# The value projections of a hybrid attention encoder in two groups of 512 columns instead of three of 384, 384 and 256

## The chip, the core and the metric

The kernel runs on one core of a Trainium2 chip. The metric is device time in microseconds of one execution, here the median of three runs. The engines are named as the profile names them: PE (TensorE, matrix products; PEld is its loading of weights), DVE (VectorE), ACT (ScalarE), POOL (GpSimd) and SP (SyncE, which issues the loads).

## The reference

Two layers over 256 tokens of width 1024, in float32. Each layer is a feed-forward block at half weight, a token-mixing block and a second feed-forward block, each with an RMS norm ahead of it and one behind it. The mixing block has one input projection that is split into three groups of heads: A (6 heads, banded attention with a bias), B (4 heads, differential attention) and C (6 heads, stick-breaking attention).

```python
proj = h @ w_in
sizes = [WIDTH_A, WIDTH_A, WIDTH_A, B_QK_WIDTH, B_QK_WIDTH, WIDTH_B, WIDTH_C, WIDTH_C, WIDTH_C]
qa, ka, va, qb, kb, vb, qc, kc, vc = jnp.split(proj, [int(c) for c in np.cumsum(sizes)[:-1]], axis=-1)
o_a = chunk_band_attention(qa.reshape(hd_a), ka.reshape(hd_a), va.reshape(hd_a), rel_bias)
...
o_b = diff_attention(qb.reshape(hd_bqk), kb.reshape(hd_bqk), vb.reshape(b, s, N_HEADS_B, DIFF_V_DIM),
                     lam, subln_g, lambda_init)
...
o_c = stick_breaking_attention(qc.reshape(hd_c), kc.reshape(hd_c), vc.reshape(hd_c))
y = jnp.concatenate([o_a.reshape(b, s, WIDTH_A), o_b.reshape(b, s, WIDTH_B),
                     o_c.reshape(b, s, WIDTH_C)], axis=-1)
return y @ w_out
```

The values va (384 columns), vb (256) and vc (384) are 1024 columns together.

## The kernel before

**Split products.** Each float32 product is made of three passes of rounded operands: a weight is cut into a rounded part (`whi`, by ACT, line 136) and the rest (`wlo`, the difference, by DVE, line 137), the activations likewise, and `mm3` (lines 366 to 368) multiplies high by high, high by low and low by high. Activations stand transposed in `xT`, K-tile by K-tile (8 of them), for two token tiles of 128 tokens.

**The stream of weights.** `Stream` holds all weights of the kernel as a list of chunks of up to 1152 columns, in the order of their use. `load` fetches a chunk into one of four raw buffers from SP's queue. `ahead(n)` issues the cutting of the next n half chunks, each one cast on ACT and one subtraction on DVE; when a chunk's second half has been cut, the chunk four places behind it is loaded. It stops where nine chunks are cut and not yet used (up to three more, "spare", lie in tiles that the feed-forward block has left free, in the trace under the names hh and hl). `done` gives a chunk back. All this is issued in program order: each engine takes its instructions in the order in which the code issued them, so where `ahead` stands in the code decides what a cast stands behind on ACT and a subtraction on DVE.

**The values.** In a mixing block of the first layer the values take chunks 66 to 73: chunks of 3, 3 and 2 K-tiles for C, the same for A, and two of 4 K-tiles for B. `values(g, t)` multiplies one group for one token tile into a PSUM tile (`pv`, named in the order of instructions by layer, group and token tile, so pv0_1_0 is layer 0, group 1, tile 0) and copies it to `v`, on ACT, for group 1 on DVE. The order is group 0 tile 0, group 1 tile 0, group 0 tile 1, group 1 tile 1, group 2 for both. In group 1 tile 0, ahead of its last chunk, `turn1` is called: it transposes the second token tile's normed activations (`pt`, line 361) and splits them into `xT` (lines 304 and 305).

**The projections and the attention.** Sixteen tiles of queries and keys follow (`pp`, chunks 74 to 89 in the first layer, one chunk of 128 columns each), and the heads' attention is dealt out among them by a table, `PLAN`: each tile has four slots, numbered through from 0 to 63, and an event at 15.4 is issued behind the matmuls of slot 15. Names used below: the first two B heads' scores `s_b` and softmaxes `p_b` (lines 854, 855, 830, 832) stand in slot 15 and those of the other two in slot 24; `wT_b` is the copy on ACT of a head's transposed weights (line 844) and `o_b` the product with the values that reads it (line 884); `z_c` and `yb` are a pair of C heads (lines 778 to 786). `PLAN["pieces"]` has the argument of `ahead` for each slot:

```python
"pieces": [
    1, 0, 0, 1, 2, 0, 3, 0, 0, 2, 1, 0, 2, 0, 0, 4, 0, 0, 0, 4, 0, 0, 2, 2, 2, 1, 0, 2, 4, 3, 1, 1, 1,
```

Of the kernel before, what the change touches and what calls it, by code (L numbers as in the profile page):

```python
# [9 lines left out]
F32 = mybir.dt.float32  # L10
# [6 lines left out]
P = 128  # L17
# [8 lines left out]
QA, KA, VA = 0, 384, 768  # L26
QB, KB, VB = 1152, 1408, 1664
QC, KC, VC = 1920, 2304, 2688
YA, YB, YC = 0, 384, 640
EPS = 1e-6  # L30
NEG = -1e30
FAR = 1e30
# [128 lines left out]
def trunk_kernel(  # L161
    ctx: ExitStack,
    tc: tile.TileContext,
    x, x_cols, f1_pre, f1_gate, f1_up, f1_down, f1_post,
    m_pre, w_in, rel_map, lq1, lk1, lq2, lk2, sub_g, w_out, m_post,
    f2_pre, f2_gate, f2_up, f2_down, f2_post,
    out,
):
    nc = tc.nc
# [8 lines left out]
    psum = ctx.enter_context(tc.tile_pool(name="psum", bufs=4, space=bass.MemoryType.PSUM))  # L178
# [40 lines left out]
    stream = Stream(nc, raw_pool, split_pool)  # L219

    def rows(ap, l, k0, k1, c0, c1):
        return ap[l, k0 * P : k1 * P, c0:c1].rearrange("(k p) n -> p k n", p=P)
# [13 lines left out]
        for k in range(KF):  # L236
            stream.add(rows(down, l, k, k + 1, 0, D), 1, D)

    V_CUTS = ((0, 3), (3, 6), (6, 8))
    QK_TILES = (  # L240
        [c for j in range(2) for c in (QB + j * P, KB + j * P)]
        + [c for j in range(3) for c in (QC + j * P, KC + j * P)]
# [2 lines left out]
    OUT_ORDER = [5, 6, 7, 3, 4, 0, 1, 2]  # L245

    def plan_mix(l):
        for c in (VC, VA):
            for k0, k1 in V_CUTS:
                stream.add(rows(w_in, l, k0, k1, c, c + 384), k1 - k0, 384)  # L250
        for h in range(2):
            stream.add(rows(w_in, l, 4 * h, 4 * h + 4, VB, VB + 256), 4, 256)
        for c in QK_TILES:
            stream.add(rows(w_in, l, 0, KT, c, c + P), KT, P)
        for k in OUT_ORDER:
            stream.add(rows(w_out, l, k, k + 1, 0, D), 1, D)
# [110 lines left out]
        nc.tensor.matmul(ps, lhsT=ah, rhs=bl, start=False, stop=False)  # L367
        nc.tensor.matmul(ps, lhsT=al, rhs=bh, start=False, stop=last)  # L368

    def tokens_out(ps, chunks, t, between=None):  # L370

        k, total = 0, sum(stream.src[c][1] for c in chunks)
        for c in chunks:
            if between and c == chunks[-1]:
                between()
            wh, wl = stream.get(c)
            for j in range(stream.src[c][1]):
                mm3(ps, xT[:, k, 0, t, :], xT[:, k, 1, t, :], wh[:, j, :], wl[:, j, :], k == 0, k == total - 1)
                k += 1

    def cols_out(ps, c, quarter=lambda q: None):

        wh, wl = stream.get(c)
        for k in range(KT):
            mm3(ps, wh[:, k, :], wl[:, k, :], xT[:, k, 0], xT[:, k, 1], k == 0, k == KT - 1)
            if k % 2:
                quarter(k // 2)
# [298 lines left out]
    def mix(i, l, turn1):  # L686
        lam_init = 0.8 - 0.6 * math.exp(-0.3 * l)
        v = act.tile([P, 2, D], F32, tag="bigl2", name=f"v{l}")
        big2 = act.tile([P, 6, SEQ], F32, tag="bigh2", name=f"big2_{l}")
        alibi, dist, dneg = big2[:, :NH_B, :], big2[:, 4, :], big2[:, 5, :]  # L690
# [10 lines left out]
        def make_lambda():  # L701
            for m in range(2):
# [9 lines left out]


        c = stream.used
        vgroups = [(YC, [c, c + 1, c + 2], 384, "acc"), (YA, [c + 3, c + 4, c + 5], 384, "acc"),
                   (YB, [c + 6, c + 7], 256, "rot")]

        def values(g, t, between=None):
            y0, chunks, n, tag = vgroups[g]
            pv = psum.tile([P, 512], F32, tag=tag, name=f"pv{l}_{g}_{t}")  # L720
            tokens_out(pv[:, :n], chunks, t, between)
            (nc.scalar.copy if g != 1 else nc.vector.tensor_copy)(v[:, t, y0 : y0 + n], pv[:, :n])

        values(0, 0)
        stream.ahead(2)
        values(1, 0, turn1)
        stream.ahead(2)
        nc.scalar.preload_act_table_set("natural_log_exp_and_others")
        values(0, 1)
        stream.done(3)  # L730
        stream.ahead(6)
        values(1, 1)
        stream.done(3)
        stream.ahead(6)
        values(2, 0)
        values(2, 1)
        stream.done(2)
        stream.ahead(6)
        qkT = act.tile([P, 16, SEQ], F32, tag="bigh1", name=f"qkT{l}")
        yb = act.tile([P, 2816], F32, tag="bigl1", name=f"yb{l}")  # L740
        yB = yb[:, :512].rearrange("p (t d) -> p t d", t=2)
# [11 lines left out]
        def pair_c(j):  # L753


            nm = f"c{l}_{j}"
            fq, fk = 4 + 2 * j, 5 + 2 * j
            zt = work.tile([P, D], F32, tag=("xg", "gpre")[j % 2], bufs=1, name=f"z_{nm}")
            z = zt[:, :768]
            if j % 2:  # L760
                e = work.tile([P, D], F32, tag="fg", bufs=1, name=f"e_{nm}")[:, :768]
            else:
                e = yb[:, 2048:2816]


            def cuts(x):
                return x[:, :512].rearrange("p (h t) -> p h t", h=2), x[:, 512:768].rearrange("p (h t) -> p h t", h=2)

            z0, z1 = cuts(z)
            for h in range(2):  # L770
                b = 64 * h
                q, k = qkT[b : b + 64, fq, :], qkT[b : b + 64, fk, :]
                s = psum.tile([P, 384], F32, tag="acc", name=f"s_{nm}_{h}")
                nc.tensor.matmul(s[:, 0:256], lhsT=k[:, 0:P], rhs=q, start=True, stop=True)
                nc.tensor.matmul(s[:, 256:384], lhsT=k[:, P:SEQ], rhs=q[:, P:SEQ], start=True, stop=True)

                diag = zt[:, 256 * h :][:, : 2 * (512 - 128 * h)].rearrange("p (b t) -> p b t", b=2)[:, :, :P]
                nc.vector.tensor_add(diag, s.rearrange("p (b t) -> p b t", t=P)[:, 0:3:2, :],
                                     negmask.unsqueeze(1).broadcast_to([P, 2, P]))
                nc.vector.tensor_copy(z0[:, h, P:], s[:, P:256])  # L780
                yield
            nc.scalar.activation(e, z, AF.Abs)
            nc.scalar.activation(e, e, AF.Exp, scale=-1.0)
            nc.scalar.activation(e, e, AF.Ln, bias=1.0)
            yield
            nc.vector.scalar_tensor_tensor(e, z, 0.0, e, ALU.max, ALU.add)
            yield
            h0 = work.tile([P, 512], F32R, tag="ta", bufs=TA, name=f"h0_{nm}")
            l0 = work.tile([P, 512], F32R, tag="tc", bufs=3, name=f"l0_{nm}")
            hl1 = work.tile([P, 512], F32R, tag="tb", bufs=3, name=f"hl1_{nm}")  # L790
            h1, l1 = hl1[:, :256], hl1[:, 256:]
            nc.scalar.copy(h1, e[:, 512:])
            nc.scalar.copy(h0, e[:, :512])
            nc.vector.tensor_sub(l1, e[:, 512:], h1.bitcast(F32))
            nc.vector.tensor_sub(l0, e[:, :512], h0.bitcast(F32))
            yield
            u1 = psum.tile([P, 256], F32, tag="acc", name=f"u1_{nm}")
            nc.tensor.matmul(u1, lhsT=tri, rhs=h1, start=True, stop=False)
            nc.tensor.matmul(u1, lhsT=tri, rhs=l1, start=False, stop=True)
            u0 = psum.tile([P, 512], F32, tag="acc", name=f"u0_{nm}")  # L800
            nc.tensor.matmul(u0, lhsT=tri, rhs=h0, start=True, stop=False)
            nc.tensor.matmul(u0, lhsT=tri, rhs=l0, start=False, stop=False)
            late = u0.rearrange("p (h t) -> p h t", h=2)[:, :, P:]
            for x, stop in ((h1, False), (l1, True)):
                nc.tensor.matmul(late, lhsT=ones_r, rhs=x.rearrange("p (h t) -> p h t", h=2), start=False, stop=stop)
            yield
            nc.vector.tensor_sub(z[:, 512:], z[:, 512:], u1)
            nc.vector.tensor_sub(z[:, :512], z[:, :512], u0)
            yield
            nc.scalar.activation(e, z, AF.Exp)  # L810
            yield
            o = psum.tile([P, SEQ], F32, tag=where("oC"), name=f"o_{nm}")
            e0, e1 = cuts(e)
            for h in range(2):
                vs = slice(YC + 64 * (2 * j + h), YC + 64 * (2 * j + h) + 64)
                columns_out(o, h, v[:, :, vs], e0[:, h, :], e1[:, h, :])
            yield
            if not yC:

                yC.append(act.tile([P, 6, SEQ], F32R, tag="bigh2", name=f"yC{l}"))  # L820
            split_copy(yC[0][:, j, :], yC[0][:, 3 + j, :], o)
            yield
# [35 lines left out]
        def head_b(h):  # L858
            fq, fk = 2 * (h // 2), 2 * (h // 2) + 1
            ps = []  # L860
# [14 lines left out]
                nc.vector.scalar_tensor_tensor(p0[:, a:b], p1[:, a:b], fac[:, t : t + 1], p0[:, a:b],  # L875
                                               ALU.mult, ALU.add)
            yield
            vs = slice(YB + 64 * h, YB + 64 * h + 64)
            pT = turned(f"b{l}_{h}", p0)
            yield  # L880
            w = turned_copy(f"b{l}_{h}", pT)
# [26 lines left out]
        def pair_a(j):  # L908
# [9 lines left out]
            ps = [soft(nms[m], ss[m], biasA[:, 2 * j + m, :], "ta") for m in range(2)]  # L918
# [10 lines left out]
            yield  # L929
            o = psum.tile([P, SEQ], F32, tag="rot", name=f"o_{nms[0]}")  # L930
            for m in range(2):
                vs = slice(YA + 64 * (2 * j + m), YA + 64 * (2 * j + m) + 64)
                columns_out(o, m, v[:, :, vs], ws[m][:, 0:2, :], ws[m][:, 2, :])
            yield
            keep_y(j, o)
# [94 lines left out]

_INS = [
    "x", "x_cols", "ffn1_pre_g", "ffn1_w_gate", "ffn1_w_up", "ffn1_w_down", "ffn1_post_g",
    "mix_pre_g", "w_in", "rel_map", "diff_lambda_q1", "diff_lambda_k1", "diff_lambda_q2",
    "diff_lambda_k2", "diff_subln_g", "w_out", "mix_post_g",
    "ffn2_pre_g", "ffn2_w_gate", "ffn2_w_up", "ffn2_w_down", "ffn2_post_g",
]
# [31 lines left out]
```

## Time and profile before

| | |
|---|---|
| median of three runs | 1001.77 us (1001.66 to 1001.86) |
| the profiled execution | 1001.47 us |
| its span, first to last instruction | 999.8 us |
| mean granted TensorE clock | 0.999 |
| PE, DVE, ACT busy | 984.4, 686.4, 584.4 us |
| loads of w_in | 48 (36 of 512, 8 of 576, 4 of 384 KB) |
| value stage of the first layer, first value matmul to first `pp` matmul | 196.82 to 220.71 us |

All times below are microseconds from the start of the span, unless marked otherwise. A row of the timeline has the start, the duration, the engine, the line, the operation with the tiles written and read, and how many alike were merged; in brackets stands how long the engine had been idle and what ended that. The durations of matmuls overlap; the spacing of their starts is what one costs.

### The profile page before, as it was taken

The numbers are of one execution on the slowest core, as the hardware profiler recorded it, in microseconds if no ns is written. First come the engines' busy times: TensorE is split into PE (matmuls) and PEld (weight loads), VectorE is DVE, ScalarE is ACT, GpSimd is POOL, SyncE is SP. The second block draws the span as 40 slices with busy tenths as digits, with TensorE's granted clock in tenths as the row PEclk, the third lists the DMA queues.
The fourth block names the chain that finished last, engine by engine and source line by source line (L and its number), as shares of the span: only waits on it lengthen the run. The fifth ranks groups of instructions, "written<-read, shape, count | busy, mean of one in ns | idle before, by whom it ended". The sixth has DMA issues, their size and how long they took to land.

```text
span 999.8 us, 16010 instructions
## 1 busy us (share of the span) xinstructions
PE 984.4 (98%) x5914; PEld 868.0 (87%) x5914; DVE 686.4 (69%) x1373; ACT 584.4 (58%) x1262; POOL 39.9 (4%) x68
## 2 busy tenths in 40 slices
PE   9999999999999999999999999999999999999997
PEld 8888888899878988888898888888998799888885
DVE  5788885668876587774567776656688657776642
ACT  5566564467766475664456666455587756655531
POOL 5000000000001000000020000001001010000000
PEclk9999999999999999999999999999999999999999
DMA  8777668566443586557646756663844516865631
GB/s 233 192 224 238 183 220 295 146 183 208 125 134 115 176 251 212 171 197 223 190 112 212 247 173 204 216 193 104 248 148 144 181 49 193 256 189 205 211 106 42
DMA packets 151326, 183.69 MB, mean 184 GB/s; under 512 B 5808, under 2 KB 134960, under 8 KB 151248
## 3 DMA queue, kind: packets, MB, share of 16 engines
q1 hardware_dynamic: 149632, 178.28, 57.3%
q0 software_dynamic: 1328, 3.87, 1.7%
q8 instruction: 46, 0.75, 0.3%
q10 hardware_dynamic: 288, 0.52, 0.1%
q14 instruction: 32, 0.26, 0.1%
HBM read 181.60 MB, written 1.05 MB: 183 GB/s over the span
## 4 chain that ended last, share of the span: by engine, by line
PE 79%; DVE 11%; ACT 6%; issue 2%; DMA 1%; POOL 0%; SPq 0%; POOLq 0%; DVEq 0%; ACTq 0%
PE pg L391 11%; PE pu L391 11%; PE acc L366 9%; PE acc L368 9%; PE acc L367 9%; PE pu L396 6%; PE pg L396 6%; DVE wlo L137 6%; PE pu L368 1%; PE pu L367 1%; PE pu L366 1%; PE pg L368 1%; PE pp L366 1%; PE pg L366 1%; PE pg L367 1%
## 5 line engine op out<-in xcount | busy, mean ns | idle before, releaser
L137 DVE TENSOR_TENSOR wlo<-raw,whi 128x512 fp32r<-128x512 f32 x630 | 399.0, 688 | 139.1 <-ACT whi L136 138.6
L136 ACT CAST whi<-raw 128x512 fp32r<-128x512 f32 x630 | 348.8, 616 | 97.6 <-PE acc L368 61.2
L391 PE MATMUL pg<-xT,whi 128*128 128x512 f32 x576 | 145.2, 394 | 1.4 <-DVE sg L402 0.7
L391 PE MATMUL pu<-xT,whi 128*128 128x512 f32 x576 | 144.3, 392 | 0.4 <-DVE h L402 0.4
L366 PE MATMUL acc<-whi,hh 128*128 128x512 f32 x352 | 137.2, 390 | 0.0
L367 PE MATMUL acc<-wlo,hh 128*128 128x512 f32 x352 | 137.0, 389 | 0.0
L368 PE MATMUL acc<-whi,hl 128*128 128x512 f32 x352 | 137.0, 389 | 0.0
L391 PEld LDWEIGHTS pg<-xT,whi 128*128 128x128 f32 x576 | 103.2, 189 | 20.9 <-ACT whi L136 1.5
L391 PEld LDWEIGHTS pu<-xT,whi 128*128 128x128 f32 x576 | 103.6, 189 | 19.2 <-DVE h L402 0.6
L396 PEld LDWEIGHTS pg<-xT,wlo 128*128 128x128 f32 x576 | 78.6, 190 | 5.6
L396 PEld LDWEIGHTS pu<-xT,wlo 128*128 128x128 f32 x576 | 78.6, 190 | 5.6
L396 PE MATMUL pu<-xT,wlo 128*128 128x256 f32 x576 | 80.3, 282 | 0.0
L396 PE MATMUL pg<-xT,wlo 128*128 128x256 f32 x576 | 80.3, 282 | 0.0
L368 PEld LDWEIGHTS acc<-whi,hl 128*128 128x128 f32 x352 | 66.1, 188 | 13.8
L367 PEld LDWEIGHTS acc<-wlo,hh 128*128 128x128 f32 x352 | 66.1, 188 | 13.5
L366 PEld LDWEIGHTS acc<-whi,hh 128*128 128x128 f32 x352 | 66.1, 188 | 13.5
L366 PE MATMUL pp<-xT,whi 128*128 128x256 f32 x256 | 76.0, 297 | 0.0
L367 PE MATMUL pp<-xT,whi 128*128 128x256 f32 x256 | 72.3, 282 | 0.0
L368 PE MATMUL pp<-xT,wlo 128*128 128x256 f32 x256 | 72.3, 282 | 0.0
L304 ACT CAST hh<-h 128x512 fp32r<-128x512 f32 x38 | 23.6, 621 | 64.1 <-DVE h L661 61.8
L366 PEld LDWEIGHTS pp<-xT,whi 128*128 128x128 f32 x256 | 48.8, 191 | 4.7 <-issue 4.0
L367 PEld LDWEIGHTS pp<-xT,whi 128*128 128x128 f32 x256 | 48.9, 191 | 0.0
(276 smaller groups left out, 1428.2 us busy)
## 6 DMA issues: line engine op xcount, KB each, us to landing
raw<-in_ffn_w_up_dram SPq DMA_DIRECT2D x88, 512.0 KB, 4.7
raw<-in_ffn_w_down_dram SPq DMA_DIRECT2D x88, 512.0 KB, 4.3
raw<-in_ffn_w_gate_dram SPq DMA_DIRECT2D x86, 512.0 KB, 4.8
raw<-in_w_in_dram SPq DMA_DIRECT2D x36, 512.0 KB, 5.4
raw<-in_w_out_dram SPq DMA_DIRECT2D x16, 512.0 KB, 3.6
raw<-in_w_in_dram SPq DMA_DIRECT2D x8, 576.0 KB, 4.4
raw<-in_w_in_dram SPq DMA_DIRECT2D x4, 384.0 KB, 3.7
yb<-in_rel_map_dram SPq DMA_DIRECT2D x2, 768.0 KB, 7.2
```

Of the source, the lines that this page charges most:

```text
L136: self.nc.scalar.copy(self.hi[:, a:b], raw[:, a:b])
L137: (lo or self.nc.vector).tensor_sub(self.lo[:, a:b], raw[:, a:b], self.hi.bitcast(F32)[:, a:b])
L304: nc.scalar.copy(hi, src)
L366: nc.tensor.matmul(ps, lhsT=ah, rhs=bh, start=first, stop=False)
L367: nc.tensor.matmul(ps, lhsT=ah, rhs=bl, start=False, stop=False)
L368: nc.tensor.matmul(ps, lhsT=al, rhs=bh, start=False, stop=last)
L391: nc.tensor.matmul(ps.rearrange("p a t -> p (a t)"), lhsT=wh[:, k % 4, cs], rhs=xT[:, k].rearrange("p a t c -> p (a t c)"), start=k == 0, ...
L396: nc.tensor.matmul(ps[:, 1, :], lhsT=wl[:, k % 4, cs], rhs=xT[:, k, 0].rearrange("p t c -> p (t c)"), start=False, stop=k == KT - 1)
```

## The change

A second weight tensor, `w_val`, is laid out on the host with the value columns of C, B and A side by side. The values are taken in two groups of 512 columns per token tile, each from four chunks of 2 K-tiles by 512 columns, so that all eight chunks have 1024 columns. `v` is laid out C, B, A. In the second token tile a chunk is given back as soon as it is used. The calls of `ahead` among the values change: after group 0 tile 0 two half chunks as before; none after group 1 tile 0; six after group 0 tile 1; four after group 1 tile 1. `PLAN` is unchanged.

```diff
-YA, YB, YC = 0, 384, 640
+VYC, VYB, VYA = 0, 384, 640
...
-    V_CUTS = ((0, 3), (3, 6), (6, 8))
...
     def plan_mix(l):
-        for c in (VC, VA):
-            for k0, k1 in V_CUTS:
-                stream.add(rows(w_in, l, k0, k1, c, c + 384), k1 - k0, 384)
-        for h in range(2):
-            stream.add(rows(w_in, l, 4 * h, 4 * h + 4, VB, VB + 256), 4, 256)
+        for g in range(2):
+            for q in range(4):
+                stream.add(rows(w_val, l, 2 * q, 2 * q + 2, 512 * g, 512 * g + 512), 2, 512)
...
-    def tokens_out(ps, chunks, t, between=None):
+    def tokens_out(ps, chunks, t, between=None, last=False):
...
                 k += 1
+            if last:
+                stream.done()
...
-        vgroups = [(YC, [c, c + 1, c + 2], 384, "acc"), (YA, [c + 3, c + 4, c + 5], 384, "acc"),
-                   (YB, [c + 6, c + 7], 256, "rot")]
 
         def values(g, t, between=None):
-            y0, chunks, n, tag = vgroups[g]
-            pv = psum.tile([P, 512], F32, tag=tag, name=f"pv{l}_{g}_{t}")
-            tokens_out(pv[:, :n], chunks, t, between)
-            (nc.scalar.copy if g != 1 else nc.vector.tensor_copy)(v[:, t, y0 : y0 + n], pv[:, :n])
+            pv = psum.tile([P, 512], F32, tag="acc", name=f"pv{l}_{g}_{t}")
+            tokens_out(pv, list(range(c + 4 * g, c + 4 * g + 4)), t, between, t == 1)
+            (nc.vector.tensor_copy if g else nc.scalar.copy)(v[:, t, 512 * g : 512 * g + 512], pv)
 
         values(0, 0)
         stream.ahead(2)
         values(1, 0, turn1)
-        stream.ahead(2)
         nc.scalar.preload_act_table_set("natural_log_exp_and_others")
         values(0, 1)
-        stream.done(3)
         stream.ahead(6)
         values(1, 1)
-        stream.done(3)
-        stream.ahead(6)
-        values(2, 0)
-        values(2, 1)
-        stream.done(2)
-        stream.ahead(6)
+        stream.ahead(4)
...
+    w_in = _np.asarray(inputs["w_in"])
+    w_val = _np.concatenate([w_in[:, :, VC : VC + 384], w_in[:, :, VB : VB + 256], w_in[:, :, VA : VA + 384]], axis=2)
```

The order of instructions on ACT, at the value copy of group 0 tile 1 in the first layer, before (line, operation, tiles; whi74 is the cast of chunk 74, x2 its two halves):

```order
L136 CAST whi74_2190<-raw74_1961 128x512 x2
L728 ACT_TABLE_LOAD
L722 COPY v0_2113<-pv0_0_1_2199 128x384
L136 CAST whi75_2225<-raw75_1973 128x512 x2
L136 CAST whi76_2233<-raw76_2111 128x512 x2
L136 CAST whi77_2241<-raw77_2148 128x512 x2
L136 CAST whi78_2275<-raw78_2196 128x512 x2
L136 CAST whi79_2283<-raw79_2231 128x512 x2
L136 CAST whi80_2291<-raw80_2239 128x512 x2
L722 COPY v0_2113<-pv0_2_0_2299 128x256
```

The same place with the change:

```order
L725 ACT_TABLE_LOAD
L720 COPY v0_2113<-pv0_0_1_2191 128x512
L137 CAST whi74_2217<-raw74_1961 128x512 x2
L137 CAST whi75_2225<-raw75_1973 128x512 x2
L137 CAST whi76_2233<-raw76_2111 128x512 x2
L137 CAST whi77_2267<-raw77_2148 128x512 x2
L137 CAST whi78_2275<-raw78_2223 128x512 x2
L137 CAST whi79_2298<-raw79_2231 128x512 x2
```

Chunk 74's casts have moved from ahead of that copy to behind it, and 79 and later ones are now issued by the slots of the projections.

The order on ACT in slots 15 to 24, from the last exponential of the first two B heads to the first one of the other two, before:

```order
L832 ACTIVATE p_b0_1_1_2539,st_b0_1_1_2540<-p_b0_1_1_2539,st_b0_1_1_2540 128x256
L136 CAST whi86_2559<-raw86_2365 128x512 x2
L953 COPY qkT0_2367<-pp0_3_2475 128x256
L951 ACTIVATE qkT0_2367<-pp0_4_2567 128x256
L136 CAST whi87_2594<-raw87_2413 128x512 x2
L953 COPY qkT0_2367<-pp0_5_2602 128x256
L136 CAST whi88_2629<-raw88_2454 128x512 x2
L832 ACTIVATE p_b0_2_0_2650,st_b0_2_0_2651<-p_b0_2_0_2650,st_b0_2_0_2651 128x128
```

The same place with the change:

```order
L823 ACTIVATE p_b0_1_1_2479,st_b0_1_1_2480<-p_b0_1_1_2479,st_b0_1_1_2480 128x256
L137 CAST whi85_2499<-raw85_2357 128x512 x2
L137 CAST whi86_2507<-raw86_2386 128x512 x2
L944 COPY qkT0_2283<-pp0_3_2415 128x256
L942 ACTIVATE qkT0_2283<-pp0_4_2515 128x256
L137 CAST whi87_2542<-raw87_2400 128x512 x2
L944 COPY qkT0_2283<-pp0_5_2550 128x256
L137 CAST whi88_2577<-raw88_2428 128x512 x2
L823 ACTIVATE p_b0_2_0_2598,st_b0_2_0_2599<-p_b0_2_0_2598,st_b0_2_0_2599 128x128
```

Chunk 85, which was cut ahead of these heads' softmaxes before, is now cut between them and the next; from chunk 86 on the order is the same. DVE's subtractions stand in the same places of its own order.

More of the change, by code (lines that the diff above doesn't have):

```diff
@@ L164, in trunk_kernel @@
     x, x_cols, f1_pre, f1_gate, f1_up, f1_down, f1_post,
-    m_pre, w_in, rel_map, lq1, lk1, lq2, lk2, sub_g, w_out, m_post,
+    m_pre, w_in, w_val, rel_map, lq1, lk1, lq2, lk2, sub_g, w_out, m_post,
     f2_pre, f2_gate, f2_up, f2_down, f2_post,
@@ L814, in pair_c @@
             for h in range(2):
-                vs = slice(YC + 64 * (2 * j + h), YC + 64 * (2 * j + h) + 64)
+                vs = slice(VYC + 64 * (2 * j + h), VYC + 64 * (2 * j + h) + 64)
                 columns_out(o, h, v[:, :, vs], e0[:, h, :], e1[:, h, :])
@@ L877, in head_b @@
             yield
-            vs = slice(YB + 64 * h, YB + 64 * h + 64)
+            vs = slice(VYB + 64 * h, VYB + 64 * h + 64)
             pT = turned(f"b{l}_{h}", p0)
@@ L931, in pair_a @@
             for m in range(2):
-                vs = slice(YA + 64 * (2 * j + m), YA + 64 * (2 * j + m) + 64)
+                vs = slice(VYA + 64 * (2 * j + m), VYA + 64 * (2 * j + m) + 64)
                 columns_out(o, m, v[:, :, vs], ws[m][:, 0:2, :], ws[m][:, 2, :])
@@ L1032 @@
     "x", "x_cols", "ffn1_pre_g", "ffn1_w_gate", "ffn1_w_up", "ffn1_w_down", "ffn1_post_g",
-    "mix_pre_g", "w_in", "rel_map", "diff_lambda_q1", "diff_lambda_k1", "diff_lambda_q2",
+    "mix_pre_g", "w_in", "w_val", "rel_map", "diff_lambda_q1", "diff_lambda_k1", "diff_lambda_q2",
     "diff_lambda_k2", "diff_subln_g", "w_out", "mix_post_g",
@@ L1053 @@
     x_cols = _np.concatenate([_np.asarray(inputs["ffn1_pre_g"])[0].reshape(KT, P).T, x_rows], axis=1)
-    inputs = dict(inputs, x_cols=x_cols, rel_map=rb[:, :, dist].transpose(0, 2, 1, 3))
+    w_in = _np.asarray(inputs["w_in"])
+    w_val = _np.concatenate([w_in[:, :, VC : VC + 384], w_in[:, :, VB : VB + 256], w_in[:, :, VA : VA + 384]], axis=2)
+    inputs = dict(inputs, x_cols=x_cols, w_val=w_val, rel_map=rb[:, :, dist].transpose(0, 2, 1, 3))
     arrays, args = {}, []
```

## The prediction

> **What bounds the kernel now.** I read the page's totals first, then TensorE's instructions through the first mixing layer, then ScalarE, VectorE and the load queue there, and last the chain of work that ended last, to see which engine's lateness reaches the end.
>
> ```profile
> span 999.8 us, 16010 instructions
> PE 984.4 (98%) x5914; PEld 868.0 (87%) x5914; DVE 686.4 (69%) x1373; ACT 584.4 (58%) x1262; POOL 39.9 (4%) x68
> PE 79%; DVE 11%; ACT 6%; issue 2%; DMA 1%; POOL 0%; SPq 0%; POOLq 0%; DVEq 0%; ACTq 0%
> ```
>
> TensorE is busy 98% of the span, yet 17% of the chain lies on VectorE and ScalarE. So TensorE is the bound on average, and there are places where the other two set the pace. The change touches one of each: the value products, which TensorE sets, and the cutting of weights behind them.
>
> **TensorE in the value stage.** The rows are from the timeline (start, duration, line, operation; in brackets idle time and what ended it).
>
> ```profile
> 184.82 0.39 PE L368 MATMUL acc<-whi,hl 128*128 128x512 f32 x1
> ...
> 194.34 0.39 PE L368 MATMUL acc<-whi,hl 128*128 128x512 f32 x1
> ...
> 196.82 0.33 PE L366 MATMUL pv<-whi,xT 128*128 128x384 f32 x1
> ...
> 204.13 1.03 PE L361 MATMUL pt<-ident,xg 128*128 128x128 f32 x8
> 204.92 0.42 PE L366 MATMUL pv<-hh,xT 128*128 128x384 f32 x1
> ...
> 206.25 0.33 PE L367 MATMUL pv<-wlo,xT 128*128 128x384 f32 x1
> 206.88 0.44 PE L368 MATMUL pv<-whi,xT 128*128 128x384 f32 x1 [0.30 <-DVE xT L305]
> 207.16 0.34 PE L366 MATMUL pv<-whi,xT 128*128 128x384 f32 x1
> ...
> 210.81 0.33 PE L366 MATMUL pv<-hh,xT 128*128 128x384 f32 x1
> ...
> 214.97 0.28 PE L366 MATMUL pv<-whi,xT 128*128 128x256 f32 x1
> ...
> 220.71 0.28 PE L366 MATMUL pp<-xT,whi 128*128 128x256 f32 x1
> ```
>
> Durations overlap, so I take spacings of starts. 42 matmuls of 512 columns lie between 184.82 and 194.34: 226.7 ns each. 45 of 384 lie between 207.16 and 214.97: 173.6 ns. 48 of 256 lie between 214.97 and 220.71: 119.6 ns. The stage runs from 196.82 to 220.71, 23.89 us.
>
> *Edit 1, two groups of 512 in place of 384, 384, 256.* A K-tile of a token tile costs three passes of 2 x 173.6 + 119.6 = 466.8 ns now and 2 x 226.7 = 453.4 ns then. With 8 K-tiles, 2 token tiles and 3 passes that is 48 x 13.4 ns = 0.64 us less in a layer.
>
> [...]
>
> *Edit 2, the stall at the turn.* The eight transposes at 204.13 give the second token tile; TensorE then has only the last chunk's six matmuls of 384 columns (1.04 us) before it needs the result, and waits: 206.25 to 206.88 is 0.63 in place of 0.17, a loss of 0.46. Then six matmuls of 512 (1.36 us) stand there, and ScalarE has no casts left ahead of the turned tile, since the turn comes 2.2 us later for it. I take the stall as gone. Together: 96 x 226.7 ns + 0.79 for the transposes = 22.55 us, so TensorE is through with the values at 219.37, **1.34 us earlier** than now (0.64 and 0.46, and 0.24 of smaller hesitations around the turn, what is left of 23.89 after 96 x 173.6 ns, 5.74, 0.79 and 0.46). From both sides: 0.64 if the stall stays, 1.34 if it goes.
>
> *Edit 3, chunks 72 and 73 are needed sooner.* The first token tile's two groups now run through all eight chunks before one is freed. Chunk 73 is wanted after the transposes, at 196.82 + 42 x 0.2267 + 0.79 = 207.13.
>
> ```profile
> 204.28 1.14 ACT L136 CAST whi<-raw 128x512 fp32r<-128x512 f32 x2
> 204.93 1.29 DVE L137 TENSOR_TENSOR wlo<-raw,whi 128x512 fp32r<-128x512 f32 x2 [0.20 <-ACT whi L136]
> ```
>
> These two rows are chunk 73's cutting now. It ends at 206.22, and 0.12 later behind a wider copy: 0.8 us to spare, cost nothing. Descriptors of 2 KB against 1.5 and 1 KB cost and bring nothing either: the eight value chunks have landed before the stage begins.
>
> **The cutting behind it.** *Edit 4, the calls to cut ahead.* This is where I expect the time to go. Before, chunk 74 is cut ahead of the copy of pv0_0_1 and chunks 75 to 80 behind it; the change puts the first cut after that copy and cuts one chunk less by every point up to slot 15 of the projections.
>
> ```profile
> 211.00 0.48 ACT L722 COPY v<-pv 128x384 f32<-128x384 f32 x1 [2.28 <-PE pv L368]
> 211.38 4.26 ACT L136 CAST whi<-raw 128x512 fp32r<-128x512 f32 x8
> 213.36 0.37 SPq L108 DMA_DIRECT2D raw<-in_w_in_dram  x1
> 217.15 1.14 ACT L136 CAST whi<-raw 128x512 fp32r<-128x512 f32 x2 [1.51 <-DMA raw<-in_w_in_dram]
> 219.97 1.14 ACT L136 CAST whi<-raw 128x512 fp32r<-128x512 f32 x2 [1.68 <-DMA raw<-in_w_in_dram]
> 221.81 1.15 ACT L136 CAST whi<-raw 128x512 fp32r<-128x512 f32 x2 [0.15 <-DMA raw<-in_w_in_dram]
> 223.61 1.14 ACT L136 CAST whi<-raw 128x512 fp32r<-128x512 f32 x2 [0.65 <-DMA raw<-in_w_in_dram]
> 225.37 1.14 ACT L136 CAST whi<-raw 128x512 fp32r<-128x512 f32 x2 [0.62 <-DMA raw<-in_w_in_dram]
> 227.77 1.14 ACT L136 CAST whi<-raw 128x512 fp32r<-128x512 f32 x2 [0.72 <-DMA raw<-in_w_in_dram]
> 230.31 1.12 ACT L136 CAST whi<-raw 128x512 fp32r<-128x512 f32 x2
> 231.56 0.68 DVE L137 TENSOR_TENSOR wlo<-raw,whi 128x512 fp32r<-128x512 f32 x1
> 233.40 0.29 DVE L830 CUSTOM_DVE_ANT_0 p_b<-s_b,big 128x128 f32<-128x128 f32 x1 [1.15 <-PE s_b L855]
> ```
>
> There are four buffers for raw chunks, so chunk n+4 is loaded only when chunk n is cut. The copy of pv0_0_1 starts 0.19 after TensorE's next matmul (210.81 to 211.00), and everything cut behind it waits. The load at 213.36, of chunk 79, follows 1.98 after the first cast; from 217.15 on chunks 79 to 84 are each cast when they land, spaced 2.82, 1.84, 1.80, 1.76 and 2.40, mean 2.12: a train that the transfers pace, as the window shows (last columns: DMA share and GB/s).
>
> ```profile
> 214.70:229.40 14.70, 14.70 (x124) 14.70 (x123) 11.29 (x22) 8.88 (x18) 0.31 (x1) 1.00 1.09 285
> ```
>
> After: pv0_0_1 is computed from 208.49 to 213.93 (24 x 0.2267), its copy starts at 214.12 and takes 0.38 x 512/384 = 0.50, so casting begins at 214.62, 3.24 after 211.38. The same train leaves 3.24 later, and its first load is chunk 78, not 79. What chunk 85 meets now, chunk 84 meets then. Chunk 85 is one more spacing behind 227.77, at 229.9 with the mean; 84 then lands at 233.1, and VectorE is through with it 1.93 later (230.31 to the end of the row at 231.56), at 235.1; with the shortest spacing, 1.76, at 234.7. Behind it in VectorE's queue stand the softmaxes of the first heads, which start now at 233.40 as soon as TensorE's scores are there and then at 234.7 to 235.1: I take **1.5 us later**. From both sides: 1.34 earlier, if the train catches up and only the scores decide; 2.6 later, if one spacing more is like the longest.
>
> *Edit 5, one chunk more in the busy part.* In slot 15 the change cuts 85 and 86 where only 86 was cut, between the first heads' softmaxes and the next ones.
>
> ```profile
> 238.81 3.69 DVE L137 TENSOR_TENSOR wlo<-raw,whi 128x512 fp32r<-128x512 f32 x6
> 242.42 0.28 DVE L830 CUSTOM_DVE_ANT_0 p_b<-s_b,big 128x128 f32<-128x128 f32 x1
> ```
>
> Six subtractions run back to back into the next softmax, 0.615 us each; two more make **1.23 us**. The next softmaxes start 1.5 + 1.23 = 2.7 us later.
>
> **Where it lands.** From the chain and the timeline:
>
> ```profile
> 232.39 0.45 PE s_b L854 x8
> ...
> 247.92 1.29 DVE wlo L137 x2
> ...
> 253.32 0.47 ACT L844 COPY wT_b<-pT_b 128x384 f32<-128x384 f32 x1
> ...
> 253.84 0.43 PE L884 MATMUL o_b<-v,wT_b 128*128 128x64 f32 x2 [0.86 <-ACT wT_b L844]
> ...
> 277.39 0.28 ACT qkT L951
> 277.72 0.55 PE pT_a L839 x3
> ```
>
> Between 232.39 and 277.39 the chain holds no TensorE work: it is the softmaxes, the cuts and the stick-breaking on VectorE and ScalarE. TensorE waits 0.86 us at o_b for a copy behind them. If that copy is 2.7 us late, o_b starts at 256.5; the 1.34 us that TensorE gained become waiting there, and every projection queued behind o_b is 2.7 us late too. I see nothing behind that gives it back, since the same work follows on all engines. The second layer is built alike:
>
> ```profile
> 723.98 0.45 PE s_b L854 x8
> 730.38 3.69 DVE wlo L137 x6
> PE o_b L884 <- ACT wT_b L844: 0.9, 1, 0.9
> ```
>
> So 2 x 2.7 = **5.4 us more**. The profiled execution took 1001.47 us, 1.67 over its span; it would take 1006.9. It stands 0.3 under the median of the runs, 1001.77, and against that I predict **1007.2 us**.
>
> **Rivals.**
> *A: the lateness never reaches TensorE, and the change is faster.* It takes that VectorE has room for the late train and the two subtractions. For it speak the idle 1.15 us at 233.40 and TensorE's 98%; against it the six subtractions that run into the softmax at 242.42, and the 0.86 us at o_b. From the point where wT_b is ready when TensorE arrives at o_b, the gain shows in full: 2 x 1.34 = 2.7, 999.1 us; 2 x 0.64 with the stall left, 1000.5.
> *B: the train catches up, only the extra chunk stays.* Then the softmaxes start when the scores do, 1.34 earlier, and 1.23 is given back: 0.1 a layer, 1001.6 us. It needs chunk 84 cut by 232.1, 2.6 to 3.0 us faster than the train's spacings give. [...]
> *C: the train is worse.* One more long spacing of 2.82 in place of 1.76 makes 1.1 more a layer, 2 x 3.8 = 7.6: 1009.4 us.
> *D: wide matmuls are dearer with these operands than in the down projection.* The row of 512 columns has the same kinds of operands, so I give it nothing of its own.
>
> **The numbers.** Main case, 1004 to 1009.5 us: 0.67. B and the cases between it and the main one, 1001.5 to 1004: 0.15. A: 0.12. Worse than 1009.5: 0.06. The range 1001.5 to 1009.5 holds 0.82; the main case's own is 1004 to 1009.5. By 0.2% (2.0 us, about what runs of this kernel can tell from no change), faster means under 999.8: 0.12; slower, over 1003.8: 0.73; between: 0.15.
>
> **What would show it.** Right: pv matmuls 0.227 us apart and no idle row at the turn; the first pp matmul near 219.4; the first long cast group near 214.6; VectorE's first p_b row near 234.9 without idle time before it; eight wlo in a row ahead of the next p_b near 245; o_b of the third or fourth head near 256.5 with 1 to 3 us of TensorE idle in that stretch. Wrong: p_b starting near 232.1 with idle time before it (A or B), or loads that land under 1.8 us apart from the first on. I am wrong in sign if ScalarE and VectorE show idle time between 234 and 253 that takes up the two subtractions.

## The result, and the profile after

The changed kernel takes 1008.27 us (median of four runs, 1007.63 to 1009.93), the kernel before 1001.71 in the same comparison: a ratio of 1.0067, 95% interval 1.0054 to 1.0079. That is 6.6 us slower, where 1007.2 was predicted. Its profiled execution took 1008.23 us, its span 1006.5. The page's totals and its chain by engine:

```profile
span 1006.5 us, 15814 instructions
PE 986.5 (98%) x5818; PEld 863.0 (86%) x5818; DVE 687.9 (68%) x1373; ACT 584.2 (58%) x1258; POOL 39.9 (4%) x68
PE 77%; DVE 11%; ACT 6%; DMA 4%; issue 2%; POOL 0%; SPq 0%; POOLq 0%; DVEq 0%; ACTq 0%
```

TensorE has 96 matmuls less and is busy 2.1 us longer. DMA's share of the chain has risen from 1 to 4%, TensorE's has fallen from 79 to 77%.

One caution on the times below. In this execution the value stage starts 0.55 us later than in the one before (first `pv` at 197.37, not 196.82). Experiments 1, 2 and 4, which run the same program up to there, start the transposes ahead of it at 194.51, 194.74 and 194.69, where it was 194.57 before and 195.12 here; so I take the 0.55 for a variation between executions and give differences in the first layer less 0.55, called net.

TensorE in the value stage, from the timeline:

```profile
197.37 0.39 PE L364 MATMUL pv<-whi,xT 128*128 128x512 f32 x1
...
206.89 1.04 PE L359 MATMUL pt<-ident,xg 128*128 128x128 f32 x8
207.68 0.47 PE L364 MATMUL pv<-whi,xT 128*128 128x512 f32 x1
208.00 0.39 PE L365 MATMUL pv<-wlo,xT 128*128 128x512 f32 x1
...
220.03 0.28 PE L364 MATMUL pp<-xT,whi 128*128 128x256 f32 x1
```

42 matmuls lie between 197.37 and 206.89, 226.7 ns each. No row near the turn has idle time in front. The stage takes 22.66 us, where it took 23.89: TensorE does gain 1.23.

ScalarE from the value copy to the next softmaxes, from the timeline:

```profile
214.79 0.59 ACT L720 COPY v<-pv 128x512 f32<-128x512 f32 x1 [4.89 <-PE pv L366]
215.28 4.26 ACT L137 CAST whi<-raw 128x512 fp32r<-128x512 f32 x8
221.04 1.14 ACT L137 CAST whi<-raw 128x512 fp32r<-128x512 f32 x2 [1.50 <-DMA raw<-in_w_in_dram]
223.89 1.14 ACT L137 CAST whi<-raw 128x512 fp32r<-128x512 f32 x2 [1.71 <-DMA raw<-in_w_in_dram]
225.62 1.14 ACT L137 CAST whi<-raw 128x512 fp32r<-128x512 f32 x2 [0.59 <-DMA raw<-in_w_in_dram]
...
233.85 1.14 ACT L137 CAST whi<-raw 128x512 fp32r<-128x512 f32 x2 [0.27 <-DMA raw<-in_w_in_dram]
...
239.57 2.16 ACT L137 CAST whi<-raw 128x512 fp32r<-128x512 f32 x4
241.64 0.36 ACT L944 COPY qkT<-pp 128x256 f32<-128x256 f32 x1
```

ScalarE stands idle for 4.89 us with nothing to cast in its program until `pv0_0_1` is done. Then the train of loads runs as late as was worked out: chunks 78 to 84 are cast as they land, at 221.02 to 233.77, 2.13 us apart in the mean (2.85 and 2.92 the longest, the others 1.72 to 1.81). VectorE behind it:

```profile
234.50 1.29 DVE L138 TENSOR_TENSOR wlo<-raw,whi 128x512 fp32r<-128x512 f32 x2 [0.44 <-ACT whi L137]
235.71 0.28 DVE L821 CUSTOM_DVE_ANT_0 p_b<-s_b,big 128x128 f32<-128x128 f32 x1
...
241.12 4.90 DVE L138 TENSOR_TENSOR wlo<-raw,whi 128x512 fp32r<-128x512 f32 x8
245.94 0.28 DVE L821 CUSTOM_DVE_ANT_0 p_b<-s_b,big 128x128 f32<-128x128 f32 x1
...
252.66 0.42 DVE L769 TENSOR_TENSOR z_c<-s_c,negmask 128x256 f32<-128x256 f32 x1
```

The first softmax starts 235.71 instead of 233.40, 1.76 later net, and no longer waits for scores. Eight subtractions stand before the next one instead of six; it starts 2.97 later net. `z_c` started here before:

```profile
249.13 0.42 DVE L778 TENSOR_TENSOR z_c<-s_c,negmask 128x256 f32<-128x256 f32 x1
```

It is 2.98 later net, and so is the end of the layer (its last transposes 317.54, not 314.00). The second layer adds 3.2.

The chain shows the loads as the start of it all:

```profile
219.66 5.94 DMA raw<-in_w_in_dram
...
227.60 6.17 DMA raw<-in_w_in_dram
233.85 0.63 ACT whi L137
...
236.04 2.03 ACT p_b L823 x9
...
243.53 2.49 DVE wlo L138 x4
```

What was not foreseen is where TensorE waits for them. TensorE's long waits in the first layer, then those in the second (total, times, longest):

```profile
PE s_b L845 <- ACT qkT L944: 2.8, 1, 2.8
...
PE s_b L845 <- ACT qkT L944: 3.0, 1, 3.0
PE o_b L875 <- ACT wT_b L835: 0.9, 1, 0.9
```

And its timeline in the first layer, at that wait and at the `o_b` that waited before:

```profile
242.05 0.83 PE L845 MATMUL s_b<-qkT 32*128 32x128 f32 x8 [2.80 <-ACT qkT L944]
...
257.55 0.33 PE L875 MATMUL o_b<-v,wT_b 128*128 128x64 f32 x2
```

It waits for the copy of the fourth projection into `qkT` (241.64 above), which ScalarE reaches only behind the four casts of slot 15. And shortly before that wait ends, at 242.05, the clock falls. Busy times by stretch of the first layer (length, PE, PEld, DVE, ACT, POOL, granted clock, DMA share, GB/s):

```profile
238.00:241.74 3.74, 1.25 (x11) 1.04 (x9) 2.87 (x14) 3.74 (x13) 0.00 (x0) 1.00 0.34 99
241.74:248.57 6.83, 6.52 (x39) 5.87 (x40) 6.58 (x25) 5.17 (x18) 0.00 (x0) 0.50 0.72 212
248.57:255.00 6.43, 6.43 (x56) 6.15 (x56) 4.60 (x15) 4.50 (x13) 0.00 (x0) 1.00 0.74 266
```

The granted clock is 0.50 for 6.83 us; in the second layer it was for 3.41. This is a part of why TensorE is counted as busier on a longer span (986.5 us, where the second experiment, with the same matmuls and no such fall, has 982.4): 39 matmuls in 6.83 us count as work there, and 56 in the 6.43 after. Both the wait and the clock invite the reading that they are the loss. The fourth experiment, read in its first layer, and the clock of single runs say they are not.

### The profile page after: what moved, and what is told of

The parts are those of the page before. It is cut to its first block, busy times and chain, and to the rows that moved or that the text cites. A ratio compares the mean times of both kernels' runs of the same rounds, so it can differ in the third digit from the quotient of the medians.

```text
span 1006.5 us, 15814 instructions
## 1 busy us (share of the span) xinstructions
PE 986.5 (98%) x5818; PEld 863.0 (86%) x5818; DVE 687.9 (68%) x1373; ACT 584.2 (58%) x1258; POOL 39.9 (4%) x68
## 4 chain that ended last, share of the span: by engine, by line
PE 77%; DVE 11%; ACT 6%; DMA 4%; issue 2%; POOL 0%; SPq 0%; POOLq 0%; DVEq 0%; ACTq 0%
PE pg L392 11%; PE pu L392 11%; PE acc L364 9%; PE acc L366 9%; PE acc L365 9%; DVE wlo L138 6%; PE pu L397 6%; PE pg L397 6%; DMA raw<-in_w_in_dram 2%; ACT whi L137 2%; PE pu L366 1%; PE pu L365 1%; PE pu L364 1%; PE pg L366 1%; PE pg L364 1%
## 5 line engine op out<-in xcount | busy, mean ns | idle before, releaser
L364 PE MATMUL pp<-xT,whi 128*128 128x256 f32 x256 | 77.5, 303 | 0.0
L365 PE MATMUL pp<-xT,whi 128*128 128x256 f32 x256 | 73.4, 287 | 0.0
L364 PEld LDWEIGHTS pp<-xT,whi 128*128 128x128 f32 x256 | 50.0, 195 | 5.5 <-issue 4.7
L365 PEld LDWEIGHTS pp<-xT,whi 128*128 128x128 f32 x256 | 50.1, 196 | 0.1
```

Source lines behind the costliest of these rows:

```text
L364: nc.tensor.matmul(ps, lhsT=ah, rhs=bh, start=first, stop=False)
```

## The experiments

All are compared over five rounds with the kernel before, which took 1001.53 us beside the first four and 1001.50 beside the last three.

**1. The cutting ahead restored in number, not in time.** The changed kernel with as many chunks cut ahead of the projections as before, so that slot 15 cuts one chunk again. Chunk 74 is cut ahead of the copy of `pv0_0_1`, as it was before (its casts start at 207.88). Chunk 75 and those behind it, and with them the train of loads, still wait for that copy: the long group of casts starts at 214.66, where it was 211.38 before.

```diff
         values(1, 0, turn1)
+        stream.ahead(2)
         nc.scalar.preload_act_table_set("natural_log_exp_and_others")
...
         values(1, 1)
-        stream.ahead(4)
+        stream.ahead(10)
```

> The changed kernel, with chunk 74 cut ahead of the copy of pv0_0_1 and chunks up to 82 ahead of slot 0, as before the change; the train of loads still leaves only after that copy. My theory (the train 3.24 us later, plus one chunk in slot 15): the first heads' softmaxes still start about 1.5 to 1.8 us later than in the kernel before, but only six subtractions stand ahead of the next ones, so 2 x 1.7 more than before: about 1005.2 us, some 3 us faster than the change. If only the chunk in slot 15 mattered: the time of the kernel before, 1001.7, or less by TensorE's 1.34 a layer. If neither matters: 1008.3 as the change.

Measured: 1005.25 us, ratio 1.0040 (1.0026 to 1.0054).

```profile
234.96 0.28 DVE L822 CUSTOM_DVE_ANT_0 p_b<-s_b,big 128x128 f32<-128x128 f32 x1
...
240.36 3.69 DVE L138 TENSOR_TENSOR wlo<-raw,whi 128x512 fp32r<-128x512 f32 x6
```

The first softmax is still late and does not wait for scores (no bracket), and six subtractions stand behind it. So the late train is worth some 3.7 us of the 6.6 by itself, with the value stage's gain already in it.

**2. All of it cut early.** The changed kernel with four chunks cut in the gap in which ScalarE stood idle for 4.89 us, ahead of the copy of `pv0_0_1`.

```diff
         nc.scalar.preload_act_table_set("natural_log_exp_and_others")
+        stream.ahead(8)
         values(0, 1)
```

> The changed kernel, with chunks 74 to 77 cut between the turn and the copy of pv0_0_1, where ScalarE and VectorE stand idle in the trace of the change (208.6 to 214.8 and 209.4 to 215.9 us). My theory: the train leaves near 211 instead of 217, VectorE waits for the scores again in slot 15, and TensorE's 1.34 us a layer come through: 999.1 to 999.6 us, and the first softmax starts at 232.1. If the wide matmuls or the layout of the values cost the time, or the early load of the kernel: 1005 us or more.

Measured: 999.01 us, ratio 0.9975 (0.9965 to 0.9985): faster than the kernel before. ScalarE, then VectorE:

```profile
209.54 4.27 ACT L137 CAST whi<-raw 128x512 fp32r<-128x512 f32 x8
215.36 1.14 ACT L137 CAST whi<-raw 128x512 fp32r<-128x512 f32 x2 [0.35 <-DMA raw<-in_w_in_dram]
...
232.33 0.29 DVE L822 CUSTOM_DVE_ANT_0 p_b<-s_b,big 128x128 f32<-128x128 f32 x1 [0.76 <-PE s_b L847]
237.74 3.69 DVE L138 TENSOR_TENSOR wlo<-raw,whi 128x512 fp32r<-128x512 f32 x6
...
248.07 0.42 DVE L770 TENSOR_TENSOR z_c<-s_c,negmask 128x256 f32<-128x256 f32 x1
```

The casts start 5.7 us earlier than in the changed kernel, the first softmax waits for TensorE's scores again and starts at 232.33, 1.07 earlier than in the kernel before, and `z_c` follows 1.06 earlier (248.07). The value layout is a gain of about 1.2 us a layer once the cutting behind it doesn't wait for its copies.

**3. The kernel before with less cut ahead.** The kernel before with the change's calls to cut ahead: chunk 74 goes behind the copy, and one chunk less is cut by every point, so that slot 15 has two chunks. The copy itself comes as early as before (the casts behind it start at 211.56, 211.38 before).

```diff
         values(1, 0, turn1)
-        stream.ahead(2)
...
         stream.done(3)
-        stream.ahead(6)
+        stream.ahead(4)
         values(2, 0)
         values(2, 1)
         stream.done(2)
-        stream.ahead(6)
```

> The kernel before, three groups as they were, but with the change's calls to cut ahead (one chunk less cut by every point up to slot 15). TensorE's work is that of the kernel before and the train leaves when it did, one chunk behind. My theory: only the two subtractions in slot 15 are added, 1.23 us a layer: 1004.2 us (the softmaxes of the first heads start at 233.4 as before, the next ones 1.2 later). If the wide matmuls or the late copy cost all of it: 1001.7 us.

Measured: 1003.95 us, ratio 1.0024 (1.0015 to 1.0034).

```profile
233.58 0.29 DVE L828 CUSTOM_DVE_ANT_0 p_b<-s_b,big 128x128 f32<-128x128 f32 x1 [1.08 <-PE s_b L853]
238.99 4.89 DVE L137 TENSOR_TENSOR wlo<-raw,whi 128x512 fp32r<-128x512 f32 x8
```

The first softmax is on time (233.58, 233.40 before), waits 1.08 for scores, and eight subtractions follow: 2.4 us in two layers, 1.21 each, which is the price of two subtractions.

**4. The copy that TensorE waits for, put ahead of the casts.** The changed kernel with that copy's event in front of slot 15's cutting.

```diff
 "qk": [
-        7.05, 7.1, 14.05, 16.05, 19.05, 23.05, 27.05, 33.05, 35.05, 39.05, 43.05, 47.05, 53.05, 55.05,
+        7.05, 7.1, 14.05, 15.8, 19.05, 23.05, 27.05, 33.05, 35.05, 39.05, 43.05, 47.05, 53.05, 55.05,
```

> The changed kernel, with the copy of the fourth projection tile (qkT, pp0_3) issued ahead of slot 15's four half-chunk casts and not behind them. In the trace of the change TensorE waits 2.8 and 3.0 us for this copy ahead of the scores of the third and fourth head, with the granted clock at 0.5 behind that. My theory: VectorE's queue is what is late, so the wait only moves to the products behind wT_b: 1008 us, within 1 of the change. The rival (that wait and the lowered clock behind it are the loss): about 2 x 2.9 less, 1002.4 us.

Measured: 1008.91 us, ratio 1.0072 (1.0059 to 1.0085): no different from the changed kernel's 1.0067 (1.0054 to 1.0079). The first layer's waits:

```profile
PE s_c L765 <- DVE st_b L821: 2.0, 1, 2.0
PE o_b L875 <- ACT wT_b L835: 1.8, 2, 0.9
PE s_b L845 <- ACT qkT L944: 0.6, 1, 0.6
```

And the busy times and the clock there, in the columns of above:

```profile
238.00:248.00 10.00, 7.42 (x65) 6.44 (x65) 9.35 (x34) 8.36 (x28) 0.00 (x0) 1.00 0.52 161
```

The wait at `s_b` is 0.6 instead of 2.8, the clock stays at 1.00 over these 10 us, and TensorE waits the time out a little later, at `s_c`, which the expectation did not name, and at `o_b`, for VectorE and ScalarE. From the first value matmul to the last transposes the first layer takes 120.01 us; the changed kernel took 120.17 and the kernel before 117.18. The time lies with those two engines; TensorE can lose it in one place or another. DVE is busy 9.35 of these 10 us.

The second layer is less clean. There `s_b` waits 1.4 and `s_c` 2.0, and the clock falls after all. The page has it as the 8 in its row of 40 slices of the span (tenths of full clock; this slice is 730 to 756):

```profile
PEclk9999999999999999999999999999989999999999
```

From the first layer's last transposes to the end of the span this execution takes 4.65 us more than the kernel before, the changed kernel 3.2 more; whether the clock makes that difference is not shown. That the loss does not need such a fall is shown by single runs: the profiled execution of the changed kernel, with its two falls in the mixing layers, has a mean granted clock of 0.993, the kernel before 0.998 or 0.999, and the runs that have 0.998 too took 1008.31 us (the changed kernel) and 1008.91 (this one), no less than the medians.

**5. Cuts moved out of that stretch.** To use what that says: the second experiment's kernel with the cuts of slots 22 to 27 done in slot 28.

```diff
     "pieces": [
-        1, 0, 0, 1, 2, 0, 3, 0, 0, 2, 1, 0, 2, 0, 0, 4, 0, 0, 0, 4, 0, 0, 2, 2, 2, 1, 0, 2, 4, 3, 1, 1, 1,
+        1, 0, 0, 1, 2, 0, 3, 0, 0, 2, 1, 0, 2, 0, 0, 4, 0, 0, 0, 4, 0, 0, 0, 0, 0, 0, 0, 0, 4, 3, 1, 1, 1,
...
+        at(28.17, lambda: stream.ahead(4))
         for n, k in enumerate(PLAN["pieces"]):
```

> The kernel e2_lead_in_gap, with the cuts of chunks 88 and 89 taken out of slots 23 to 27 and issued in slot 28, where ScalarE casts while it waits for VectorE's z_c and VectorE subtracts while ScalarE does that pair's Abs, Exp and Ln (VectorE stands idle 2.7 us there in the kernel before). My theory (VectorE's and ScalarE's chain from slot 15 on sets when TensorE goes on): z_c starts about 2.5 us earlier, the 0.9 us of waiting at o_b goes, and with the two small waits of 0.2 some 1.1 to 1.3 us a layer are gained: 996.5 us. If TensorE's own work already sets the end there: 999.0 as e2.

Measured: 995.65 us, ratio 0.9942 (0.9929 to 0.9954). It beats both kernels.

```profile
237.60 2.49 DVE L138 TENSOR_TENSOR wlo<-raw,whi 128x512 fp32r<-128x512 f32 x4
...
245.41 0.42 DVE L770 TENSOR_TENSOR z_c<-s_c,negmask 128x256 f32<-128x256 f32 x1
...
246.47 2.49 DVE L138 TENSOR_TENSOR wlo<-raw,whi 128x512 fp32r<-128x512 f32 x4
```

Four subtractions now stand between the two groups of softmaxes, four others behind `z_c`, which starts at 245.41 instead of 248.07. The wait at `o_b` is gone. The gain over the second experiment, 1.68 us a layer, is more than the 1.1 to 1.3 I gave it; the waits that are gone, 0.9 at `o_b` and 0.2 at `o_c`, account for that much, and where the remaining 0.4 to 0.6 comes from stays open.

**6. A fifth raw buffer.** The changed kernel, with weight chunks of at most 1024 columns in place of 1152 to make room; the program is cut into other chunks elsewhere too.

```diff
-CH = 1152
-NRAW = 4
+CH = 1024
+NRAW = 5
```

> The changed kernel with five raw buffers in place of four and chunks of at most 1024 columns (all of its chunks are), so that one more chunk lies loaded when the train leaves. My theory: chunk 84 is one place further ahead in the train, the first heads' softmaxes start near 234.0 in place of 235.7 and the eight subtractions stay: 2 x (2.98 - 1.8) = 2.4 over the kernel before, about 1004 us, give or take 1 for what the fifth buffer does elsewhere. If the number of loads in flight does not matter: 1008 us.

Measured: 1003.52 us, ratio 1.0022 (1.0013 to 1.0031).

```profile
233.32 0.28 DVE L821 CUSTOM_DVE_ANT_0 p_b<-s_b,big 128x128 f32<-128x128 f32 x1
238.73 4.90 DVE L138 TENSOR_TENSOR wlo<-raw,whi 128x512 fp32r<-128x512 f32 x8
```

With one more load under way when ScalarE stands idle, the first softmax is back at 233.32, and the extra chunk in slot 15 remains. So the lateness comes from buffers that are given back late: one load more ahead of that wait takes it away.

**7. The early cutting alone, in the kernel before.**

```diff
         values(1, 0, turn1)
-        stream.ahead(2)
         nc.scalar.preload_act_table_set("natural_log_exp_and_others")
+        stream.ahead(8)
         values(0, 1)
```

> The kernel before, three groups as they were, with chunks 74 to 77 cut in the same place as in e2_lead_in_gap. My theory: in the kernel before VectorE already waits 1.15 us for the scores in slot 15, so an earlier train brings nothing: 1001.5 us, within 0.5. That makes all of e2's gain the wide groups'. If the earlier cutting is what e2 gains by: 999.0 us.

Measured: 1001.55 us, ratio 1.0000 (0.9991 to 1.0009).

```profile
233.52 0.29 DVE L830 CUSTOM_DVE_ANT_0 p_b<-s_b,big 128x128 f32<-128x128 f32 x1 [1.97 <-PE s_b L855]
```

VectorE comes to the first softmax earlier and waits 1.97 for the scores instead of 1.15. Where the scores decide, cutting earlier brings nothing; so the second experiment's gain is the value layout's and not the new place's.

Put together: the late train costs 3.7 net of the values' gain (experiment 1, 3.1 us a layer against experiment 2) and the chunk more in slot 15 costs 2.4 (experiment 3); the sum, 6.1, is near the 6.6 measured.

## Why the prediction was right, and where it was off

- *The matmuls (edits 1 and 2).* Right: 226.7 ns, no idle time at the turn, 1.23 us gained against 1.34. The first `pp` matmul at 220.03 is 219.48 net, 219.4 was given. The 0.64 us came from the measured spacings, 226.7, 173.6 and 119.6 ns. That the gain would be lost in waiting was right too; experiment 2 shows it whole.
- *Needed sooner (edit 3).* Right: nothing waits for chunk 73.
- *The late train (edit 4).* The mechanism was right and its size a little short. The casts begin at 215.28, 214.73 net (214.62 given), and the loads land at a mean of 2.13 us (2.12 was used). Chunk 84 was put at 233.1 and lands at 233.77, 233.22 net. VectorE reaches the softmax at 235.16 net. Of my span of 234.7 to 235.1 I had taken the middle, and its upper end was nearer: 1.76 us in place of 1.5, and 2.0 in the second layer. The outer bound of 2.6 does not come out of the rows: with the longest spacing, 2.82, the same sum gives 235.76, 2.4 later.
- *One chunk more (edit 5).* Right: 1.21 us by the traces and by experiment 3, 1.23 given.
- *Where it lands.* Half right. That VectorE's and ScalarE's lateness sets the end and comes out at about 2.7 a layer holds (2.98 and 3.2). The step that named `o_b` as the place of TensorE's wait failed: I followed the queue of VectorE and left out that slot 15's two casts more stand on ScalarE ahead of the copy into `qkT`, which slot 24's `s_b` reads. TensorE waits 2.8 there, then runs at a granted clock of 0.50 for 6.83 us, and no longer waits at `o_b` in the first layer, though that `o_b` is as late as was worked out (257.55, 257.00 net; 256.5 was given). Experiment 4 shows, in its first layer, that this changed the place and not the sum.
- *The sum.* 5.4 was given; the terms measure 1.76 and 1.21 in the first layer and 3.2 together in the second, 6.2. The 0.55 ahead of the value stage is the rest of the 6.7 between the two spans; the prediction has no term for it, and single runs of the changed kernel lie between 1007.63 and 1009.93.
- *The rivals.* A needed room on VectorE: it is there when the cutting is early (experiment 2, 999.01 beside A's 999.1), and not here. B needed chunk 84 cut by 232.1; its cast only starts at 233.85, the spacing is 2.13, as before, and the stretch of the train moves 266 GB/s (row below).

```profile
217.50:235.00 17.50, 17.50 (x144) 16.57 (x144) 14.27 (x31) 10.78 (x22) 0.30 (x1) 1.00 1.01 266
```

C's second long spacing did come (2.92 for the last load), but four short ones of 1.72 to 1.81 kept the mean, and its 3.8 us a layer was not reached: 2.98 and 3.2 are nearer to the 2.7 of the main case, though 1008.27 lies midway between 1007.2 and C's 1009.4.

## What to carry to other kernels

When work for later stages is interleaved by hand, the place of the interleaved call in an engine's program is part of the change: moved behind a copy that waits 4.9 us, it held the buffers, and through them the loads, the softmaxes and the end. Read each piece of a wider tile both ways, for what the wide engine saves (1.2 us a layer here) and for what now waits until the wider tile is done. And when the profile shows a striking new wait, take it away once before blaming it: here it moved, and the time stayed.

## What the runs showed of the hardware

The granted clock fell behind some of TensorE's waits and not behind others. In the changed kernel it went to 0.50 behind waits of 2.80 and 3.0 us, for 6.83 us (241.74 to 248.57) and for 3.41 us (736.67 to 740.08). In the first experiment, behind a wait of 1.61 us in the first layer, matmuls of 256 columns stand 0.12 us apart, so it did not fall there. In the fourth `s_c` waits 2.0 us in both layers: in the first the clock is 1.00 over the window that holds this wait (238 to 248), in the second the page has the 8 in the slice of these waits. So the length of the wait at `s_c` alone does not decide. In the changed kernel matmuls of 256 columns stood 0.21 us apart at 0.50, and 0.12 at 1.00:

```profile
244.05 0.42 PE L365 MATMUL pp<-xT,whi 128*128 128x256 f32 x1
244.26 0.42 PE L366 MATMUL pp<-xT,wlo 128*128 128x256 f32 x1
...
248.79 0.28 PE L364 MATMUL pp<-xT,whi 128*128 128x256 f32 x1
248.91 0.28 PE L365 MATMUL pp<-xT,whi 128*128 128x256 f32 x1
```

What decides whether the clock falls behind a wait, and for how long, these runs do not show.
